# Mixing-stage range sums moved from ScalarE to VectorE, the first layer's input forms made later, and five more blocks computed by seven products

## The chip, the cores and the metric

The kernel runs on one core of one Trainium2 chip. The metric is device time in microseconds (us) of one execution. TensorE multiplies; VectorE, ScalarE and GpSimd work on its results; each engine takes its instructions strictly in the order in which they were written, and waits at the head of its queue until what the instruction needs is there.

## What is computed

One inference step of a one-layer hybrid decoder on 264 tokens: 256 prompt tokens and 8 sampled ones with a carried state. The layer is a half-step SwiGLU (feed-forward 1), a mixing block, and a second SwiGLU (feed-forward 2); a last RMSNorm follows. The reference, cut:

```python
D_MODEL, D_FF, SEQ, DEC_BATCH, H_A, DK = 2048, 5504, 256, 8, 4, 256

def swiglu(x, wg, wu, wd):
    return (jax.nn.silu(x @ wg) * (x @ wu)) @ wd

def mixing_block(h, w_in, b_gates, conv_w, conv_b, norm_mlstm, norm_conv, w_out, C0, n0, m0, buf0):
    z = h @ w_in
    q, k, v, o, ig, fg, gb, gc, xc = jnp.split(z, offs, axis=-1)
    ...
    ha, C_f, n_f, m_f = mlstm_chunkwise(qh, kh, vh, logi, logf, C0, n0, m0)   # 4 heads
    ha = ha * lax.rsqrt(jnp.mean(ha * ha, axis=-1, keepdims=True) + EPS)
    ha = ... * norm_mlstm * jax.nn.sigmoid(o)
    u = gc * xc                                   # short gated convolution, 3 taps
    yc = sum(cw[j] * u_ext[:, j:j + S] for j in range(CONV_W)) + conv_b
    yb = gb * yc                                  # normalised per group of 128 channels
    return jnp.concatenate([ha, yb], axis=-1) @ w_out, C_f, n_f, m_f, new_buf

h = h + 0.5 * swiglu(rmsnorm(h, norm_ffn1), ffn1_gate, ffn1_up, ffn1_down)
h = h + mixing_block(rmsnorm(h, norm_mix), ...)
h = h + 0.5 * swiglu(rmsnorm(h, norm_ffn2), ffn2_gate, ffn2_up, ffn2_down)
y = rmsnorm(h, norm_final)
```

Everything is float32 in memory; the weights (some 350 MB) are read once.

## The kernel before

**Layout.** Activations are kept transposed, channels on the 128 partitions and the 264 tokens along the free dimension. A weight matrix is cut into blocks of 128 output channels. A *product* is one such block: 16 contraction steps of 128 for an input of 2048 channels, and 22 or 21 steps for one half of the 5504 feed-forward channels. Feed-forward blocks j = 0 to 42 are worked in two halves (0 to 21 and 22 to 42): gate and up products of all blocks of the half, then the *down* products, 16 output blocks in 8 pairs (`db // 2` = 0 to 7), which add the half's share into `h`.

**Split numbers.** A float32 number is scaled and cut into two float16 numbers, high and low. For the weights ScalarE casts the high part (`high`, L240) and VectorE subtracts to get the low one (`low`, L248). Each product has three matmuls per contraction step (`three`, L322 to L324): high by high, high by low, low by high, each 264 columns. A weight tile `w` holds up to 8 steps. `fetch` (L254) issues the DMA of a raw tile, the cast, and the subtraction (with `lag` set, the subtraction waits until the next fetch); there are six buffers of `wraw` and of `w`, so the cast of a tile waits until TensorE has done with the tile six before.

**By seven.** Some blocks are computed in pairs by `product_pair` (L361): gate and up of one block (`GU_SEVEN`), or two down blocks (`DOWN_SEVEN`, keyed by layer and half, listing `db // 2`). The high-by-high matmuls stay as they are (264 columns, L387). The two correction terms are replaced, for every two contraction steps, by seven products of half the tokens (132 columns, two matmuls each, L371 and L372). For that VectorE must make four sums of weight tiles per pair of tiles (`weight_sums`, L301, tile `s`), sums of the input in *forms* (`token_sums`, L359: `f` of the layer's input, `g` of the activations), and put the results together (`join`, L427 to L437; in a down pair, `joined` then adds them to `h` at L869).

**Order of the work.** There is no scheduler: the order on each engine is that of the program. `tick()` advances a counter when a product begins, `tick(0.5)` half-way through, and `at(delta, f)` files the work `f` to be issued at a later tick; a pair counts as two products. So `at(1, norm.form, 0)` puts the forms one product later on VectorE's queue, and `Head` (L1174) and `Conv` (L1488) spread a head's or a convolution block's small steps over the products that follow theirs.

**Range sums.** The float16 cut holds only for numbers within a range. `watch` (L562) sums the absolute values of the last 16 columns of each result in PSUM into a column of `stat`; `join` does the like for pairs into `twins` (L437). At the end the sums are compared with bounds, and if one is out, the whole step is done again in full float32 (`hymba_step`, L142). In this kernel `watch` is one ScalarE activation with an accumulated output (L569, tile `seen`). It is called for every gate, up and down block not computed by seven, for every projection of the mixing block (`project`, L1033, after VectorE's scaled eviction at L1036), for the gates, for the 16 output blocks (`result`, L1605), and for the last two blocks.

**Mixing.** `MIX_ORDER` (L82) interleaves four heads (6 products each), eight convolution blocks (3 each) and eight output gates. For each head, ScalarE squares 16 columns of the sampled outputs at tick 12.5 (`squares`, L1471, activation at L1473) and TensorE sums them at tick 13.5 (`norm`, L1475, through `column_sums`, L673).

Of the kernel before, what the change touches and what calls it, by code (L numbers as in the profile page):

```python
# [8 lines left out]
F32 = mybir.dt.float32  # L9
# [3 lines left out]
AF = mybir.ActivationFunctionType  # L13
ALU = mybir.AluOpType
# [36 lines left out]
GU_SEVEN = {  # L51
    n: [j for half in starts for j in half]
    for n, starts in (
        ("1", (range(7, 21, 2), range(22, NFB - 1, 2))), ("2", (range(5, 21, 2), range(22, NFB - 1, 2))),
    )
}
DOWN_SEVEN = {("1", 0): (1, 3, 5, 7), ("1", 1): (1, 3, 5), ("2", 0): (1, 3, 5, 7), ("2", 1): (1, 3)}
PAIRS = sum(len(v) for v in GU_SEVEN.values()) + sum(len(v) for v in DOWN_SEVEN.values())
TH = T // 2

# [104 lines left out]
def step(ctx: ExitStack, tc: tile.TileContext, a: dict, shared, bad=None):  # L165
# [141 lines left out]
    def at(delta, fn, *args):  # L307
        agenda.setdefault(int(seq[0]) + delta, []).append((fn, args))
# [250 lines left out]
        onesb = const.tile([128, 128], BF16, name="onesb")  # L559
        nc.gpsimd.memset(onesb, 1.0)  # L560

    def watch(ps, rows=None):  # L562

        if half_size:
            j, n = len(stats), ps.shape[-1]
            stats.append(j)
            for r in rows or [slice(0, 128)]:
                seen = tmp.tile([128, SEEN], F32, tag="seen", name="seen", bufs=2)
                nc.scalar.activation(  # L569
                    seen[r], ps[r, n - SEEN : n], AF.Abs, accum_out=stat[r, j : j + 1]  # L570
                )

    def watch_norm(ssum):
# [191 lines left out]
    def ffn(layer, norm, done, start=None, end=None):  # L765
        with ExitStack() as stack:
# [55 lines left out]
            for half, blocks in enumerate(HALVES):  # L822
                act = {}
                def block(i, j):
                    nonlocal first
                    pg = gate_up(j, "g")
                    if first:
                        norm.finish()
                        first = False
                    zg = t264("ta")  # L830
                    nc.vector.tensor_tensor(zg, pg, norm.r, op=ALU.mult)  # L831
                    watch(pg)
                    sg = t264("tb")
                    nc.scalar.activation(sg, zg, AF.Silu)
                    pu = gate_up(j, "u")
                    zu = t264("tc")
                    nc.vector.tensor_tensor(zu, pu, norm.r, op=ALU.mult)
                    activated(j, i, zu, sg)
                    watch(pu)

                for i, j in enumerate(blocks):
                    if j in sevens:
                        by_seven(j, i)
                        continue
                    if first and start is not None:

                        ps4 = start()
                        for n, ps in enumerate(ps4):
                            early[n // 2, "gu"[n % 2]] = ps
                        for step, pairs in ((0, (0, 1)), (1, (2, 3)), (1.5, (4, 5)), (2, (6, 7))):  # L850
                            at(step, norm.square_pairs, fpool, pairs)
                        tick(0)
                        for which in "gu":
                            early[2, which] = product((layer, which, 2), norm.x, range(KB))
                    if half_size and j == (3 if start is not None else 1):
                        for g in range(2):
                            at(1 + g, norm.form, g)
                    lag[0] = half_size and j >= (3 if start is not None else 1)
                    if (j, "g") in early and not first:

                        at(j / 2 + 1, block, i, j)
                        continue
                    block(i, j)
# [14 lines left out]
                for db in range(0, KB - apart, 2):  # L878
# [5 lines left out]
                    for i in (db, db + 1):  # L884
# [3 lines left out]
                        )  # L888
                        if half == 1:
                            done(i)  # L890
                        watch(ps)
                lag[0] = False
                release()
                if apart:
# [810 lines left out]
```

## Time and profile before

| | |
|---|---|
| median of three runs | 1838.57 us (1837.24, 1838.57, 6681.73) |
| profiled execution, its own time | 1840.21 us |
| span in the profile | 1838.5 us, 44896 instructions |
| mean granted TensorE clock | 0.993 of full |
| TensorE busy (matmuls) | 1798.1 us, 98% |
| VectorE busy | 1525.3 us, 83% |
| ScalarE busy | 912.0 us, 50% |
| GpSimd busy | 140.4 us, 8% |
| HBM read | 366.72 MB, 206 GB/s read and written over the span |

By stage (from the stretches of the trace; busy us):

| stage | from to us | TensorE idle | VectorE | ScalarE |
|---|---|---|---|---|
| layer 1, gate and up, first half | 0 to 238 | 4.56 | 208.63 | 125.04 |
| layer 1, down, first half | 238 to 359 | 0.00 | 101.80 | 53.68 |
| layer 1, gate and up, second half | 359 to 572 | 0.25 | 196.33 | 96.86 |
| layer 1, down, second half | 572 to 690 | 0.00 | 102.32 | 56.82 |
| mixing, projections | 690 to 1070 | 23.85 | 283.52 | 229.91 |
| mixing, output blocks | 1070 to 1150 | 0.00 | 48.48 | 39.03 |
| layer 2, gate and up, first half | 1150 to 1371 | 0.28 | 194.13 | 103.34 |
| layer 2, down, first half | 1371 to 1494 | 0.00 | 103.58 | 54.32 |
| layer 2, gate and up, second half | 1494 to 1705 | 0.24 | 194.46 | 96.12 |
| layer 2, down, second half, and the end | 1705 to 1838.5 | 11.26 | 92.07 | 56.83 |

A row of the trace gives start and duration in us, engine, line, operation, output and inputs by the program's names, and in brackets how long the engine sat idle before it and whose instruction ended that. The granted clock is the share of full speed at which TensorE was allowed to run. One of the three runs took 6681.73 us; the repeat in float32 is the one branch of the program that could add so much, but that run has no profile.

### The profile page before, as it was taken

To read this page: it belongs to the slowest core of one execution; us is meant where nothing else is said; L and a number is where in the kernel's file an instruction comes from. 1 tells how busy PE (TensorE), PEld (TensorE's weight loads), DVE (VectorE), ACT (ScalarE), POOL (GpSimd) and SP (SyncE) were. 2 spreads that over 40 slices of the span, in tenths; PEclk is the share of its full clock that TensorE was granted. 3 is DMA by queue.
4 is the path that set the end of the run, shared out by engine and by line. 5 is a ranking of instruction groups with operands and counts; after the bars stand their busy time and mean duration, and the time that the engine had idled before them with its cause. 6 is when DMAs were issued, how large, how long until landed. Compare 5 with 4: busy or idle time off the path is not lost.

```text
span 1838.5 us, 44896 instructions
## 1 busy us (share of the span) xinstructions
PE 1798.1 (98%) x18780; PEld 1600.2 (87%) x18780; DVE 1525.3 (83%) x2371; ACT 912.0 (50%) x1738; POOL 140.4 (8%) x200
## 2 busy tenths in 40 slices
PE   9999999999999999989989999999999999999997
PEld 8899889999998987877878888899988999998886
DVE  7889988899998986777777766789988899999875
ACT  7544444444444544566656654544454444444542
POOL 0000000000000232211111022000000000000131
PEclk9999999999999999999999999999999999999999
DMA  8556666666666665877767666666666666666663
GB/s 300 185 184 203 196 221 194 210 204 199 200 191 206 201 203 179 294 251 248 242 226 254 202 204 200 196 195 186 205 211 199 200 207 197 193 207 195 213 200 100
DMA packets 118517, 381.51 MB, mean 208 GB/s; under 512 B 14973, under 2 KB 24797, under 8 KB 118305
## 3 DMA queue, kind: packets, MB, share of 16 engines
q1 hardware_dynamic: 109104, 350.53, 60.0%
q0 software_dynamic: 8256, 27.57, 4.4%
q8 instruction: 149, 2.44, 0.5%
q10 hardware_dynamic: 944, 0.45, 0.1%
q14 instruction: 64, 0.52, 0.1%
HBM read 366.72 MB, written 11.78 MB: 206 GB/s over the span
## 4 chain that ended last, share of the span: by engine, by line
PE 74%; DVE 11%; ACT 7%; issue 5%; DMA 1%; SPq 0%; ACTq 0%; DVEq 0%; POOL 0%; POOLq 0%
PE ps L324 16%; PE ps L322 16%; PE ps L323 16%; PE ps L387 10%; PE ps L371 8%; PE ps L372 8%; DVE w L248 4%; ACT w L240 3%; DVE s L301 1%; ACT jk L1465 1%; DMA wraw<-in_w1gu 1%; ACT cs L1437 1%; ACT seen L569 1%; DVE jk L1457 0%; DVE qkv L1036 0%
## 5 line engine op out<-in xcount | busy, mean ns | idle before, releaser
L248 DVE SCALAR_TENSOR_TENSOR w<-wraw,w 128x1024 f16<-128x1024 f32 (+3 forms) x692 | 800.6, 1181 | 159.6 <-ACT w L240 158.3
L240 ACT ACTIVATE w<-wraw 128x1024 f16<-128x1024 f32 (+3 forms) x692 | 665.3, 1007 | 115.1 <-issue 57.6
L324 PE MATMUL ps<-x,w 128*128 128x264 f16 x1568 | 433.6, 277 | 3.3 <-DVE w L248 3.3
L322 PE MATMUL ps<-x,w 128*128 128x264 f16 x1568 | 433.6, 277 | 0.0
L323 PE MATMUL ps<-x,w 128*128 128x264 f16 x1568 | 433.5, 276 | 0.0
L324 PEld LDWEIGHTS <-w 128*128 128x128 f16 x3576 | 350.8, 98 | 63.7 <-DVE w L248 9.6
L322 PEld LDWEIGHTS <-w 128*128 128x128 f16 x3576 | 351.3, 98 | 55.1 <-ACT w L240 3.0
L323 PEld LDWEIGHTS <-w 128*128 128x128 f16 x3576 | 350.9, 98 | 53.4 <-issue 0.3
L324 PE MATMUL ps<-xm,w 128*128 128x264 f16 x896 | 249.3, 278 | 3.3 <-DVE w L248 3.3
L322 PE MATMUL ps<-xm,w 128*128 128x264 f16 x896 | 249.4, 278 | 2.5 <-ACT w L240 2.5
L323 PE MATMUL ps<-xm,w 128*128 128x264 f16 x896 | 249.3, 278 | 0.0
L322 PE MATMUL ps<-a,w 128*128 128x264 f16 (+2 forms) x856 | 227.7, 271 | 0.0
L323 PE MATMUL ps<-a,w 128*128 128x264 f16 (+2 forms) x856 | 227.7, 271 | 0.0
L324 PE MATMUL ps<-a,w 128*128 128x264 f16 (+2 forms) x856 | 227.6, 271 | 0.0
L569 ACT ACTIVATE seen<-ps 128x16 f32<-128x16 f32 (+1 forms) x214 | 37.5, 175 | 331.3 <-DVE ta L831 132.2
L387 PEld LDWEIGHTS <-w 128*128 128x128 f16 x1682 | 162.0, 98 | 22.8
L372 PEld LDWEIGHTS <-s 128*128 128x128 f16 x1672 | 162.2, 97 | 0.0
L371 PEld LDWEIGHTS <-s 128*128 128x128 f16 x1672 | 161.3, 96 | 0.0
L301 DVE TENSOR_TENSOR s<-s,w 128x1024 f16<-128x1024 f16 (+2 forms) x218 | 146.0, 670 | 3.8
L301 DVE TENSOR_TENSOR s<-w 128x1024 f16<-128x1024 f16 (+2 forms) x218 | 138.2, 675 | 4.0
L387 PE MATMUL ps<-x,w 128*128 128x264 f16 x1120 | 137.4, 276 | 0.0
L372 PEld LDWEIGHTS <-w 128*128 128x128 f16 x1264 | 123.3, 98 | 1.7
(272 smaller groups left out, 2275.1 us busy)
## 6 DMA issues: line engine op xcount, KB each, us to landing
wraw<-in_w2gu SPq DMA_DIRECT2D x172, 512.0 KB, 4.7
wraw<-in_w1gu SPq DMA_DIRECT2D x164, 512.0 KB, 4.6
wraw<-in_win SPq DMA_DIRECT2D x112, 512.0 KB, 5.2
wraw<-in_w2d SPq DMA_DIRECT2D x52, 448.0 KB, 4.1
wraw<-in_w1d SPq DMA_DIRECT2D x46, 448.0 KB, 4.0
wraw<-in_w1d SPq DMA_DIRECT2D x36, 512.0 KB, 4.5
wraw<-in_wout SPq DMA_DIRECT2D x32, 512.0 KB, 4.6
wraw<-in_w2d SPq DMA_DIRECT2D x32, 512.0 KB, 4.5
```

Source lines behind the costliest of these rows:

```text
L240: nc.scalar.activation(dst, src, AF.Copy, scale=scale)
L248: nc.vector.scalar_tensor_tensor(dst, src, scale, hi, op0=ALU.mult, op1=ALU.subtract)
L301: nc.vector.tensor_tensor(s[:, out], x, y, op=ALU.add)
L322: nc.tensor.matmul(ps, wh, xk[:, 0, :], start=first, stop=False)
L323: nc.tensor.matmul(ps, wh, xk[:, 1, :], start=False, stop=False)
L324: nc.tensor.matmul(ps, wl, xk[:, 0, :], start=False, stop=last)
L371: nc.tensor.matmul(ps, w[0], x[:, 1], start=first, stop=False)
L372: nc.tensor.matmul(ps, w[1], x[:, 0], start=False, stop=last)
L387: nc.tensor.matmul(ps[:, :T], hi[:, i], xs[i][:, 0], start=(k0 + i == 0), stop=False)
L569: nc.scalar.activation(seen[r], ps[r, n - SEEN : n], AF.Abs, accum_out=stat[r, j : j + 1])
L1437: nc.scalar.activation(c[:, b], c[:, b], AF.Copy, scale=sib[:, 2 * n + b, self.hd : self.hd + 1])
L1465: nc.scalar.activation(self.jk[n][:, b, eb], self.jk[n][:, b, eb], AF.Copy, accum_out=ha[self.hd][:, eb, col : col + 1],)
```

## The change

Four edits:

- In the mixing block, for the output blocks and for the last two blocks, `watch` becomes a VectorE reduction (absolute values, 16 columns of PSUM, `tensor_reduce`). The feed-forward blocks keep the ScalarE form by `scalar=True`.
- In layer 1 the forms of the input are filed 4 and 6 ticks after block 3 begins; they were filed 1 and 2 ticks after.
- `DOWN_SEVEN` gains the pairs that take (1, 3, 5, 7) to (1, 3, 4, 6, 7), (1, 3, 5) to (1, 3, 4, 6), and in layer 2 (1, 3) to (1, 3, 4).
- `GU_SEVEN` of layer 2 starts at block 3, not 5.

By these tables 36 gate/up blocks and 17 down pairs are computed by seven; there were 35 and 13. (The few words that name the change speak of 18 down pairs; the table lists 17.)

```diff
-        ("1", (range(7, 21, 2), range(22, NFB - 1, 2))), ("2", (range(5, 21, 2), range(22, NFB - 1, 2))),
+        ("1", (range(7, 21, 2), range(22, NFB - 1, 2))), ("2", (range(3, 21, 2), range(22, NFB - 1, 2))),
...
-DOWN_SEVEN = {("1", 0): (1, 3, 5, 7), ("1", 1): (1, 3, 5), ("2", 0): (1, 3, 5, 7), ("2", 1): (1, 3)}
+DOWN_SEVEN = {
+    ("1", 0): (1, 3, 4, 6, 7), ("1", 1): (1, 3, 4, 6),
+    ("2", 0): (1, 3, 4, 6, 7), ("2", 1): (1, 3, 4),
+}
...
-    def watch(ps, rows=None):
+    def watch(ps, rows=None, scalar=False):
...
             for r in rows or [slice(0, 128)]:
-                seen = tmp.tile([128, SEEN], F32, tag="seen", name="seen", bufs=2)
-                nc.scalar.activation(
-                    seen[r], ps[r, n - SEEN : n], AF.Abs, accum_out=stat[r, j : j + 1]
+                if scalar:
+                    seen = tmp.tile([128, SEEN], F32, tag="seen", name="seen", bufs=2)
+                    nc.scalar.activation(
+                        seen[r], ps[r, n - SEEN : n], AF.Abs, accum_out=stat[r, j : j + 1]
+                    )
+                    continue
+                nc.vector.tensor_reduce(
+                    stat[r, j : j + 1], ps[r, n - SEEN : n], axis=mybir.AxisListType.X,
+                    op=ALU.add, apply_absolute_value=True,
                 )
...
-                    watch(pg)
+                    watch(pg, scalar=True)
...
                         for g in range(2):
-                            at(1 + g, norm.form, g)
+                            at((4 + 2 * g) if start is not None else (1 + g), norm.form, g)
```

The lines of the changed kernel stand 3 to 9 further down (L569 becomes L573, L1473 becomes L1482).

**ScalarE in the mixing block, at the squares of the second head.** The names are `jk` a product of state and query that is summed, `yb` a convolution block's output, `w` a weight tile, `ex` the decays, `sq` the squares. Before:

```order
L1465 ACTIVATE jk,ha_10388<-jk 128x256 x4
L240 ACTIVATE yb_10381<-yc 128x264
L240 ACTIVATE w<-wraw 128x1024 x2
L569 ACTIVATE seen,stat<-ps 128x16
L1253 ACT_TABLE_LOAD
L1253 ACTIVATE ex<-ex 128x256
L1253 ACTIVATE ex<-ex 128x128
L240 ACTIVATE w<-wraw 128x1024 x2
L1473 ACTIVATE sq_12653<-ha_10388 128x16
L569 ACTIVATE seen,stat<-ps 128x16
```

The same place of the changed kernel:

```order
L1474 ACTIVATE jk,ha_10552<-jk 128x256 x4
L243 ACTIVATE yb_10545<-yc 128x264
L243 ACTIVATE w<-wraw 128x1024 x2
L1262 ACT_TABLE_LOAD
L1262 ACTIVATE ex<-ex 128x256
L1262 ACTIVATE ex<-ex 128x128
L243 ACTIVATE w<-wraw 128x1024 x2
L1482 ACTIVATE sq_12789<-ha_10552 128x16
```

Only the range sums (`seen`) are gone from the queue; on VectorE a reduction into `stat` now follows each eviction of a projection.

**VectorE in layer 1, between the first evictions.** `ta` and `tc` are evicted gate and up products, `a` the activations, `f` the forms. Before:

```order
L837 TENSOR_TENSOR tc<-ps,rstd 128x264
L780 TENSOR_TENSOR tc<-tc,tb 128x264
L248 SCALAR_TENSOR_TENSOR a_682<-tc,a_682 128x264
L359 TENSOR_TENSOR f_687<-x_192 128x1056 x2
L359 TENSOR_TENSOR f_687<-f_687,x_192 128x1056
L359 TENSOR_TENSOR f_687<-x_192,f_687 128x1056
L248 SCALAR_TENSOR_TENSOR w<-wraw,w 128x1024
L831 TENSOR_TENSOR ta<-ps,rstd 128x264
```

In the changed kernel the first forms stand behind the eviction of block 4's gate:

```order
L789 TENSOR_TENSOR tc<-tc,tb 128x264
L251 SCALAR_TENSOR_TENSOR w<-wraw,w 128x1024
L251 SCALAR_TENSOR_TENSOR a_682<-tc,a_682 128x264 x2
L251 SCALAR_TENSOR_TENSOR w<-wraw,w 128x1024
L840 TENSOR_TENSOR ta<-ps,rstd 128x264
L362 TENSOR_TENSOR f_915<-x_192 128x1056 x2
L362 TENSOR_TENSOR f_915<-f_915,x_192 128x1056
L362 TENSOR_TENSOR f_915<-x_192,f_915 128x1056
L251 SCALAR_TENSOR_TENSOR w<-wraw,w 128x1024 x2
```

Six weight tiles and the evictions of blocks 1 to 3 have moved ahead of the first forms; the second forms follow one block later.

**VectorE in layer 1, second down half, from the last sums of pair 3 on.** `s` are the weight sums, `y` and `twins` belong to the join of pair 3, `h` is the residual. Before, pair 4 is two ordinary products:

```order
L301 TENSOR_TENSOR s<-s,w 128x2x256 x2
L248 SCALAR_TENSOR_TENSOR w<-wraw,w 128x896 x4
L430 TENSOR_TENSOR y_9573<-y_9573,ps 128x132
L431 TENSOR_TENSOR y_9573<-ps,y_9573 128x264
L434 TENSOR_TENSOR y_9573<-ps,y_9573 128x132
L435 TENSOR_TENSOR y_9573<-ps,y_9573 128x264
L436 TENSOR_TENSOR y_9573<-ps,y_9573 128x264
L437 TENSOR_REDUCE twins<-y_9573 128x2
L869 SCALAR_TENSOR_TENSOR h_81<-y_9573,h_81 128x528
L248 SCALAR_TENSOR_TENSOR w<-wraw,w 128x896
```

In the changed kernel pair 4 is by seven too. These rows begin behind the sums of its first two tiles:

```order
L304 TENSOR_TENSOR s<-s,w 128x1024 x2
L251 SCALAR_TENSOR_TENSOR w<-wraw,w 128x1024 x2
L304 TENSOR_TENSOR s<-w 128x1024 x2
L304 TENSOR_TENSOR s<-s,w 128x1024 x2
L433 TENSOR_TENSOR y_9668<-y_9668,ps 128x132
L434 TENSOR_TENSOR y_9668<-ps,y_9668 128x264
L437 TENSOR_TENSOR y_9668<-ps,y_9668 128x132
L438 TENSOR_TENSOR y_9668<-ps,y_9668 128x264
L439 TENSOR_TENSOR y_9668<-ps,y_9668 128x264
L440 TENSOR_REDUCE twins<-y_9668 128x2
L878 SCALAR_TENSOR_TENSOR h_81<-y_9668,h_81 128x528
L251 SCALAR_TENSOR_TENSOR w<-wraw,w 128x640 x2
```

The join of pair 3 now stands between the second and the third pair of tiles of pair 4, which TensorE needs next.

More of the change, by code (lines that the diff above doesn't have):

```diff
@@ L838, in block @@
                     activated(j, i, zu, sg)
-                    watch(pu)
+                    watch(pu, scalar=True)
                 for i, j in enumerate(blocks):
@@ L890, in ffn @@
                             done(i)
-                        watch(ps)
+                        watch(ps, scalar=True)
                 lag[0] = False
```

## The prediction

> **What bounds the kernel now.** I read the page's first table, then the stretches by stage and around the dips of the granted clock (TensorE, its weight loads, VectorE, ScalarE and GpSimd busy, clock, DMA):
>
> ```profile
> PE 1798.1 (98%) x18780; PEld 1600.2 (87%) x18780; DVE 1525.3 (83%) x2371; ACT 912.0 (50%) x1738; POOL 140.4 (8%) x200
> ...
> 55.00:70.00 15.00, 12.71 (x99) 10.18 (x98) 14.27 (x21) 8.98 (x20) 0.00 (x0) 0.89 0.63 203
> 790.00:822.00 32.00, 25.74 (x199) 21.21 (x197) 23.78 (x44) 21.28 (x53) 5.43 (x11) 0.95 0.79 273
> 868.00:890.00 22.00, 16.67 (x115) 13.62 (x114) 15.57 (x33) 10.31 (x21) 3.98 (x9) 0.84 0.61 189
> 948.00:970.00 22.00, 16.75 (x128) 13.91 (x127) 15.68 (x32) 10.54 (x19) 3.98 (x9) 0.84 0.53 172
> 238.00:359.00 121.00, 121.00 (x1374) 109.78 (x1372) 101.80 (x145) 53.68 (x81) 0.00 (x0) 1.00 0.65 211
> 572.00:690.00 118.00, 118.00 (x1256) 105.67 (x1254) 102.32 (x148) 56.82 (x100) 26.51 (x29) 1.00 0.66 206
> 690.00:1070.00 380.00, 356.15 (x3024) 303.24 (x3023) 283.52 (x514) 229.91 (x543) 57.07 (x101) 0.98 0.71 237
> ```
>
> TensorE is the bound: in the down stages it never rests, so only fewer matmuls help there. In the mixing block's projections it rests 380 - 356.15 = 23.85 us, though VectorE (283.52) and ScalarE (229.91) are far from full: something waits, nothing is overloaded. The waits of that stage (total, times, longest):
>
> ```profile
> PE ps L673 <- ACT sq L1473: 13.3, 4, 5.3
> PE ps L324 <- DVE w L248: 3.3, 5, 0.9
> PE ps L322 <- ACT w L240: 2.5, 2, 2.3
> ...
> DVE w L248 <- ACT w L240: 75.7, 48, 3.4
> ACT seen L569 <- DVE qkv L1036: 74.0, 24, 7.6
> ```
>
> ScalarE and VectorE wait for each other. One round of it, from the timelines around the stall at 870:
>
> ```profile
> 863.43 0.18 ACT L569 ACTIVATE seen<-ps 128x16 f32<-128x16 f32 x1 [4.35 <-DVE qkv L1036]
> 865.51 1.99 ACT L240 ACTIVATE w<-wraw 128x1024 f16<-128x1024 f32 x2
> 871.57 0.18 ACT L569 ACTIVATE seen<-ps 128x16 f32<-128x16 f32 x1 [4.07 <-DVE qkv L1036]
> 871.89 1.28 ACT L1253 ACT_TABLE_LOAD   x1
> 875.60 0.20 ACT L1473 ACTIVATE sq<-ha 128x16 f32<-128x16 f32 x1
> ...
> 866.59 2.36 DVE L248 SCALAR_TENSOR_TENSOR w<-wraw,w 128x1024 f16<-128x1024 f32 x2 [3.25 <-ACT w L240]
> 870.84 0.29 DVE L1249 TENSOR_TENSOR ex<-ex,bc 128x128 f32<-128x128 f32 x1
> 871.05 0.42 DVE L1036 TENSOR_TENSOR qkv<-ps,rstd 128x264 f32<-128x264 f32 x1
> ...
> 875.85 1.02 PE L673 MATMUL ps<-sq,ones 128*128 128x8 f32 x4 [5.33 <-ACT sq L1473]
> ```
>
> `seen` waits for VectorE's eviction, the casts stand behind `seen`, VectorE's subtractions wait for the casts, and the next eviction stands behind those. From one `seen` to the next is 871.57 - 863.43 = 8.14 us, for one projection. TensorE needs less for one, by the pieces of the chain of waits where it never stops:
>
> ```profile
> 87.81 1.80 PE ps L387 x16
> 92.83 1.80 PE ps L387 x16
> 108.65 1.80 PE ps L387 x16
> ```
>
> 16 matmuls of 264 columns take 1.80, so 0.1125 each, and a projection of 48 takes 5.4. ScalarE thus falls 2.7 us behind with such a round, until the squares are late and TensorE stands 5.33 us.
>
> **What a stall costs besides.** After the stalls the clock is below 1. Lost are, by the four stretches, (1 - 0.89) x 15 = 1.65, 0.05 x 32 = 1.6, and 0.16 x 22 = 3.5 twice; 8.6 of it in the mixing block. The Trainium skill, "TensorE: Matmul & The Clock Gate" (Part 1), has the clock halved after at least one idle window of about 3.4 us. Here the 2.29 us of 57 (its row is below) sufficed. By the page's length the first two of the four losses would not hang on their gaps and would stay, and the sum would be 3.3 us smaller; I go by the rows.
>
> **The range sums.** They leave ScalarE's queue; with `seen` gone the circle is cut, since neither a cast nor anything behind it waits for the eviction any more. ScalarE still waits for VectorE at `ex`, at the products `jk` and the convolution's inputs, but those were issued half a projection to one and a half earlier. For 870: without the waits of 4.35 and 4.07, `sq` is held by `ex`, which ended at 871.13 behind 3.25 us of waiting for casts; 867.9, then exponentials and casts as now (from the table load's end at 873.17 to 875.60, 2.4) give 870.3, against TensorE's asking at 870.52. It is just in time, with no credit for earlier rounds. I take away the squares' 13.3, the casts' 2.5, half of the subtractions' 3.3, and the clock's 8.6, and leave 0.5 a head, 2.0, for squares still late: 13.3 + 2.5 + 1.6 + 8.6 - 2.0 = 24.0.
>
> VectorE gets 58 reductions in this stage (56 projections, two for the gates). None of this form is in the trace. Nearest are
>
> ```profile
> L437 DVE TENSOR_REDUCE twins<-y 128x2 f32<-128x32 f32 x48 | 9.0, 188 | 1.6
> L592 DVE TENSOR_REDUCE downs<-ps 128x1 f32<-128x264 f32 x8 | 3.0, 422 | 0.0
> ```
>
> in size the first, from PSUM the second, which reads 264 columns. 58 x 0.188 = 10.9, at most 58 x 0.422 = 24.5. It goes into 283.5 of now 350 us, so up to 308 (88%): hidden, except where VectorE is last. I charge 2.0, some ten of them, and 0 to 10.9 for the range. Below nothing it can't be. Next late is VectorE itself, at the gates, whose part of the 23.85 (4.75, what the three waits don't hold) stays. Mixing: -24.0 + 2.0 = -22.0. The 16 sums of the output blocks and the two at the end (18 x 0.188 = 3.4) lie under matmuls; without that cover they cost that.
>
> **The forms of layer 1.** VectorE then TensorE:
>
> ```profile
> 55.32 1.32 DVE L359 TENSOR_TENSOR f<-x 128x1056 f16<-128x1056 f16 x2
> 57.29 0.71 DVE L359 TENSOR_TENSOR f<-x,f 128x1056 f16<-128x1056 f16 x1
> 57.92 1.22 DVE L248 SCALAR_TENSOR_TENSOR w<-wraw,w 128x1024 f16<-128x1024 f32 x1
> 71.65 0.43 DVE L831 TENSOR_TENSOR ta<-ps,rstd 128x264 f32<-128x264 f32 x1 [0.41 <-PE ps L324]
> ...
> 59.19 0.29 PE L324 MATMUL ps<-x,w 128*128 128x264 f16 x1 [2.29 <-DVE w L248]
> ```
>
> TensorE stands 2.29 us for the tile that is subtracted behind the second forms (55.32 to 57.92, 2.6). They and the first forms, as long, now come later, so the tile is there 2.6 to 5.2 us sooner: the stall and its 1.65 of clock go, -3.9. At 71.65 VectorE already waits for TensorE with the same work done, so the forms find room before block 7, their first user at 87.8. If not, the stall returns there at the same price.
>
> **Five more by seven.** Between 87.81 and 92.83 lies half a gate/up block by seven: 5.02, less 1.80 leaves 3.22 for 56 small matmuls, 0.0575 each. An ordinary block is 96 x 0.1125 = 10.80, one by seven 10.04: -0.76. A down pair of 22 steps: 132 x 0.1125 = 14.85 against 44 x 0.1125 + 154 x 0.0575 = 13.81, -1.04, twice; of 21 steps 14.18 against 46 x 0.1125 + 140 x 0.0575 = 13.23, -0.95, twice. Together -4.7. Their cover is VectorE's lead:
>
> ```profile
> 341.37 1.41 DVE L301 TENSOR_TENSOR s<-s,w 128x1024 f16<-128x1024 f16 x2
> 345.95 1.80 PE ps L387 x16
> 354.58 1.29 DVE L301 TENSOR_TENSOR s<-w 128x1024 f16<-128x1024 f16 x2
> 359.57 1.29 DVE L301 TENSOR_TENSOR s<-w 128x1024 f16<-128x1024 f16 x2
> 363.25 0.28 DVE L430 TENSOR_TENSOR y<-y,ps 128x132 f32<-128x132 f32 x1
> 365.76 4.62 DVE L248 SCALAR_TENSOR_TENSOR w<-wraw,w 128x1024 f16<-128x1024 f32 x4
> ...
> 630.36 0.88 DVE L301 TENSOR_TENSOR s<-s,w 128x512 f16<-128x512 f16 x2
> 631.06 0.73 PE L387 MATMUL ps<-a,w 128*128 128x264 f16 x5
> ```
>
> Sums were ready at 342.78; TensorE, starting the pair at 345.95, needs them after 1.80 and 24 x 0.0575, at 349.13: 6.3 us of lead. Subtractions and sums go at 359.57 - 354.58 = 4.99 a pair of tiles, TensorE at 5.02, so a run of sevens only loses the joins, 365.76 - 363.25 = 2.5 each. Where pairs 6 and 7 and block 22 now follow each other, two joins leave 1.3: no stall. In the second half of layer 1 the lead at the third tiles of pair 3 is smaller: sums at 631.24, needed 14 x 0.1125 + 12 x 0.0575 after 631.06, at 633.33, 2.1. One join ahead of pair 4's third tiles makes it -0.4, and the next tile's subtraction stands behind a cut of `xm`: I charge 1.5 there and 0.5 in layer 2, which cuts nothing; 0 to 6 for the range. Layer 2's block 3 uses forms made at block 1, as block 5 did. Net -2.7.
>
> **The sum.** -22.0 - 3.9 - 2.7 = -28.6 on the profiled execution's 1840.2 (span 1838.5 and 1.7 around it) gives 1811.6. That execution lay 1.6 above the median of 1838.57, so I forecast 1810.
>
> **The rivals.**
>
> *The circle loosens only.* ScalarE still waits for `ex`, `jk` and the taps; just in time at 870 may be just late. If a third of mixing's gain comes, 7.3: 1838.6 - 7.3 - 3.9 - 2.7 = 1825. Against it: 74.0 us of waiting had `seen` at its end, and the ties left reach back further.
>
> *The wait moves to VectorE.* The reductions lengthen the queue that the evictions stand in, by 10.9, and the squares stay late: mixing gives nothing, 1832. The Trainium skill, "VectorE: DVE Perf Modes" (Specifications), puts ScalarE nearer to PSUM and VectorE nearer to SBUF, which speaks for leaving the sums; no row here shows that distance. Against it: VectorE waits 75.7 us in this stage and has room for them.
>
> *VectorE becomes the bound in the down stages: slower than before.* In 238 to 359 it has 101.80; one pair more brings 2 x 4.99 + 3.8 for the short third of sums and subtractions, of which the subtractions (half) were there, and a join: some 9.5, 111 of 120. The margin of 1.3 at block 22 is the point: if sums run a fifth slower (beside GpSimd's squares, say), two pairs lose 2 x 2.8 us more and each of five places stalls 5 us and 1.7 of clock: 5 x 6.7 - 4.7 = +29. With the forms' -3.9 and a mixing block that, as in the case before, gives nothing, 1863. For it: the lead of 2.1 in the second half. Against it: 0.00 idle in these stages now.
>
> *Everything goes.* All 23.85 and 8.6 of mixing, with 3.9 and 4.7: -41, 1798. Against it: the gates' chain is VectorE's own.
>
> *The change doesn't do it.* A repeat of the whole step, should a VectorE sum fall out of its bounds, would cost thousands of us; the sums are of the same numbers. An 18th down pair, which the tables lack, would be worth about 1.0 more.
>
> **How the numbers follow.** Forecast 0.62 (1803 to 1818), loosened circle 0.18 (1819 to 1829), wait moved 0.08 (1830 to 1838), everything 0.06 (under 1803), VectorE the bound 0.05, repeat 0.01. The range takes the forecast's own and the loosened circle's, and half of "everything" below: 1801 to 1828, some 8 in 10. About 2% is what a measurement of this kernel can tell from no change; it lies at 1801.8 and 1875. Faster takes most of "everything", 0.05; slower the repeat and the tail of the VectorE case, 0.02; within, 0.93.
>
> **What would show it.** Right: the wait of L673 for the squares under 3 us, ScalarE's waits for `qkv` gone, VectorE's waits for casts in mixing well under 75.7, clock 1.00 from 868 to 970, no gap near 57 us, 17 joins in down pairs. Wrong: squares still late behind `ex`; TensorE waiting for `s` or `w` at pair 4 of layer 1's second half or at block 22; reductions much over 0.2 us.

## The result, and the profile after

The changed kernel takes 1811.72 us (median; 1811.32 to 1812.50) against 1838.57 us for the kernel before on the same chip. Two runs are left out of the medians and ratios here, one of the kernel before (6681.73 us) and one of the experiment with the first halves' tables taken back (10187.09 us), which have no profile. The ratio is 0.9856, with a 95% interval of 0.9837 to 0.9876: 26.5 us less (23 to 30), short of the 2% that were to be told from no change. The forecast was 1810 us. That the total came out is luck: three of its parts did not, and their errors cancel.

The first table of the page of the changed kernel, then its stretches around the place of the old stall at 57 us, over its mixing projections, and over its stall at 42 us (TensorE, weight loads, VectorE, ScalarE and GpSimd busy, granted clock, DMA):

```profile
PE 1784.7 (99%) x19080; PEld 1595.9 (88%) x19080; DVE 1572.0 (87%) x2528; ACT 896.0 (49%) x1571; POOL 145.9 (8%) x200
...
55.00:70.00 15.00, 15.00 (x136) 13.04 (x134) 14.41 (x23) 9.06 (x22) 0.00 (x0) 1.00 0.64 208
694.00:1031.00 337.00, 336.02 (x2934) 290.80 (x2934) 279.32 (x561) 214.72 (x419) 62.60 (x101) 1.00 0.78 263
41.00:50.00 9.00, 8.09 (x53) 6.27 (x54) 5.88 (x11) 5.26 (x11) 0.00 (x0) 0.81 0.42 130
```

TensorE now rests 337.00 - 336.02 = 0.98 us in the mixing projections, at full clock. What it waits for in the whole run of the changed kernel (total, times, longest), and VectorE's largest wait in the mixing projections:

```profile
PE ps L327 <- DVE w L251: 5.9, 9, 1.1
PE ps L682 <- DVE sq L748: 2.7, 1, 2.7
...
PE ps L390 <- ACT w L243: 1.1, 2, 0.5
PE ps L374 <- DVE s L304: 0.8, 2, 0.5
PE ps L459 <- ACT xm L243: 0.7, 1, 0.7
...
DVE w L251 <- ACT w L243: 24.5, 17, 3.4
```

The head's squares are no longer in the list. New are short waits, each at most 1.1 us, for VectorE's tiles `w` and `s`: these lie in the stages with more blocks by seven and in the second gate/up halves, which follow such stages.

The lengths of the stages, each from TensorE's first matmul that reads the stage's input to that of the next stage (for example `x` after `a` for the second gate/up half), in us:

| stage | before | after | difference | forecast |
|---|---|---|---|---|
| start and layer 1 gate/up, first half | 244.74 | 244.86 | +0.12 | -3.9 |
| layer 1 down, first half | 114.85 | 113.80 | -1.05 | -1.04 |
| layer 1 gate/up, second half | 219.63 | 222.08 | +2.45 | 0 |
| layer 1 down, second half | 110.87 | 113.25 | +2.38 | +0.55 |
| mixing projections and output blocks | 455.87 | 422.96 | -32.91 | -22 |
| layer 2 gate/up, first half | 232.42 | 232.78 | +0.36 | -0.76 |
| layer 2 down, first half | 114.85 | 113.80 | -1.05 | -1.04 |
| layer 2 gate/up, second half | 219.61 | 222.15 | +2.54 | 0 |
| layer 2 down, second half, and the end | 125.66 | 125.02 | -0.64 | -0.45 |
| span | 1838.5 | 1810.7 | -27.8 | -28.6 |

So mixing gave 10.9 us more than forecast, the five added pairs (four of down blocks, and gate and up of one block) cost 5.0 us where 2.7 were to be gained, and in this execution the first stage became no shorter.

### The profile page after: what moved, and what is told of

Same layout as the page of the kernel before. It is cut to its first block, busy times and chain, and to the rows that moved or that the text cites. A ratio compares the mean times of both kernels' runs of the same rounds, so it can differ in the third digit from the quotient of the medians.

```text
span 1810.7 us, 45495 instructions
## 1 busy us (share of the span) xinstructions
PE 1784.7 (99%) x19080; PEld 1595.9 (88%) x19080; DVE 1572.0 (87%) x2528; ACT 896.0 (49%) x1571; POOL 145.9 (8%) x200
## 3 DMA queue, kind: packets, MB, share of 16 engines
q8 instruction: 151, 2.47, 0.5%
## 4 chain that ended last, share of the span: by engine, by line
PE 74%; DVE 17%; ACT 4%; issue 3%; DMA 1%; SPq 0%; ACTq 0%; DVEq 0%
PE ps L327 17%; PE ps L325 17%; PE ps L326 17%; PE ps L390 8%; PE ps L374 7%; PE ps L375 7%; DVE w L251 6%; DVE s L304 5%; ACT w L243 3%; DMA wraw<-in_w1gu 1%; DVE g L362 1%; DVE a L251 1%; DVE y L821 1%; PE ps L682 0%; DVE y L434 0%
## 5 line engine op out<-in xcount | busy, mean ns | idle before, releaser
L327 PE MATMUL ps<-x,w 128*128 128x264 f16 x1536 | 424.9, 277 | 4.6 <-DVE w L251 4.6
L325 PE MATMUL ps<-x,w 128*128 128x264 f16 x1536 | 424.9, 277 | 0.0
L326 PE MATMUL ps<-x,w 128*128 128x264 f16 x1536 | 424.8, 277 | 0.0
L327 PEld LDWEIGHTS <-w 128*128 128x128 f16 x3372 | 330.2, 98 | 56.9 <-DVE w L251 8.5
L326 PEld LDWEIGHTS <-w 128*128 128x128 f16 x3372 | 330.2, 98 | 49.7
L325 PEld LDWEIGHTS <-w 128*128 128x128 f16 x3372 | 330.4, 98 | 48.4 <-issue 0.6
L390 PEld LDWEIGHTS <-w 128*128 128x128 f16 x1886 | 181.1, 98 | 27.0 <-ACT w L243 1.8
L374 PEld LDWEIGHTS <-s 128*128 128x128 f16 x1872 | 180.0, 96 | 2.3 <-DVE s L304 2.2
L375 PEld LDWEIGHTS <-s 128*128 128x128 f16 x1872 | 181.7, 97 | 0.0
L327 PE MATMUL ps<-a,w 128*128 128x264 f16 (+2 forms) x684 | 180.2, 269 | 1.4 <-DVE w L251 1.4
L325 PE MATMUL ps<-a,w 128*128 128x264 f16 (+2 forms) x684 | 180.2, 269 | 0.0
L326 PE MATMUL ps<-a,w 128*128 128x264 f16 (+2 forms) x684 | 180.2, 269 | 0.0
L304 DVE TENSOR_TENSOR s<-s,w 128x1024 f16<-128x1024 f16 (+2 forms) x246 | 164.8, 670 | 4.3
L304 DVE TENSOR_TENSOR s<-w 128x1024 f16<-128x1024 f16 (+2 forms) x246 | 156.5, 677 | 5.3
L390 PE MATMUL ps<-x,w 128*128 128x264 f16 x1152 | 141.8, 276 | 1.1 <-ACT w L243 1.1
L375 PEld LDWEIGHTS <-w 128*128 128x128 f16 x1418 | 138.3, 98 | 2.5 <-DVE w L251 0.4
L374 PEld LDWEIGHTS <-w 128*128 128x128 f16 x1418 | 138.1, 97 | 2.0
```

Of the source, the lines that this page charges most:

```text
L304: nc.vector.tensor_tensor(s[:, out], x, y, op=ALU.add)
L325: nc.tensor.matmul(ps, wh, xk[:, 0, :], start=first, stop=False)
L326: nc.tensor.matmul(ps, wh, xk[:, 1, :], start=False, stop=False)
L327: nc.tensor.matmul(ps, wl, xk[:, 0, :], start=False, stop=last)
L374: nc.tensor.matmul(ps, w[0], x[:, 1], start=first, stop=False)
L375: nc.tensor.matmul(ps, w[1], x[:, 0], start=False, stop=last)
```

## The experiments

Each kernel below was timed beside new runs of the kernel before on the same chip. The stages carry the arguments, since a stage without change repeats from run to run within some 0.1 us; only the start (240 to 245 us) and the mixing projections without their stall (335.7 to 339.3 us) vary more.

**Each edit alone.** The range sums only, with the feed-forward blocks kept on ScalarE as in the change:

```diff
...
-                seen = tmp.tile([128, SEEN], F32, tag="seen", name="seen", bufs=2)
-                nc.scalar.activation(
-                    seen[r], ps[r, n - SEEN : n], AF.Abs, accum_out=stat[r, j : j + 1]
+                nc.vector.tensor_reduce(
+                    stat[r, j : j + 1], ps[r, n - SEEN : n], axis=mybir.AxisListType.X,
+                    op=ALU.add, apply_absolute_value=True,
                 )
...
```

> The kernel before with the range sums of the mixing on VectorE, and nothing else of the change. Theory (the sums cut the whole circle of ScalarE's wait for the subtraction, the squares' stall and the lowered clock): the stages of the mixing and of the output blocks lose 33 us together as they do in the changed kernel, so about 1806 us. Rival (the sizes of the prediction, which left 2 us of stalls, took 2 us for the reductions, and counted half of the subtractions): -22 us, about 1817. Rival that the wait moves to VectorE: about 1838.

Measured: 1807.68 us, ratio 0.9831 (0.9814 to 0.9847), 31 us less (28 to 34). The mixing and its output blocks take 335.99 + 86.40 us where they took 367.51 + 88.36: 33.5 us less. The prediction's size of 22 is outside.

The five pairs by seven only:

```diff
-("2", (range(5, 21, 2), range(22, NFB - 1, 2))),
+("2", (range(3, 21, 2), range(22, NFB - 1, 2))),
-DOWN_SEVEN = {("1", 0): (1, 3, 5, 7), ("1", 1): (1, 3, 5), ("2", 0): (1, 3, 5, 7), ("2", 1): (1, 3)}
+DOWN_SEVEN = {("1", 0): (1, 3, 4, 6, 7), ("1", 1): (1, 3, 4, 6), ("2", 0): (1, 3, 4, 6, 7), ("2", 1): (1, 3, 4)}
```

> The kernel before with the five added pairs of blocks by seven, and nothing else of the change. Theory (a third pair in a row spends VectorE's lead, and the following half of gate/up blocks does not give it back): the profile shows 2 to 2.5 us more in the second gate/up halves and in the down blocks of the first layer's second half, 1 us less in the down blocks of the first halves, in all about +5 us: about 1843 us. Rival (the prediction): -2.7 us, about 1836 us.

Measured: 1845.03 us, ratio 1.0036 (1.0022 to 1.0051), 6.7 us more (4 to 9). The stages repeat those of the changed kernel: first down halves 113.80 and 113.81, second gate/up halves 222.09 and 222.17, layer 1's second down half 113.28.

The later forms only:

```diff
-                            at(1 + g, norm.form, g)
+                            at((4 + 2 * g) if start is not None else (1 + g), norm.form, g)
```

> The kernel before with the two forms of x later in the first layer, and nothing else of the change. Theory: the stall of 2.29 us about 57 us after the start goes, and with it the half clock behind it: -3.9 us, about 1834.7 us. Rival (the start is set by the loads of the weights, which land as late or later, and the stall only moves ahead): within 1 us of 1838.6.

Measured: 1833.67 us, ratio 0.9978 (0.9968 to 0.9987), 4.1 us less (2 to 6). Its first stage takes 240.72 us, 4.0 less than before, and in the stretch of the old stall TensorE does not rest:

```profile
55.00:70.00 15.00, 15.00 (x135) 13.04 (x134) 14.66 (x22) 9.06 (x20) 0.00 (x0) 1.00 0.70 225
```

The changed kernel without the five pairs, that is sums and forms together:

> The changed kernel with the kernel before's tables of pairs by seven (no fifth pair in any half, gate/up blocks of the second layer from block 5). Theory (the five pairs cost about 5 us net): about 1806.5 us or less, which beats the changed kernel. Rival (the prediction, the five pairs bring 2.7 us): about 1814.4 us.

Measured: 1803.74 us, ratio 0.9814 (0.9798 to 0.9831). The changed kernel came to 0.9856 (and 0.9839 when run again, below): without the pairs it is faster. Its edit is the second diff, taken back from the changed kernel.

**What the mixing block waited for.** Two kernels go out from the kernel before and leave everything but the mixing's range sums alone. One leaves these out:

```diff
         nc.vector.tensor_tensor(z, ps, nm.r, op=ALU.mult)
-        watch(ps)
         return z
```

> The kernel before with the 56 range sums of the mixing's projections left out altogether (their columns of the range test keep the value they are set to at the start, so that part of the test is not computed); those of the gates and of the output blocks stay on ScalarE. Beside the kernel with the sums alone on VectorE (ratio 0.983, projections of the mixing 336.0 us where before took 367.5) it gives the price of the 56 reductions on VectorE. Theory (ScalarE's wait was the cost and the reductions lie beside other work): 336 us again, about 1807 to 1810 us. Rival (VectorE's queue is paid for, 56 x 0.165 us): 9 us less than that kernel, 327 us for the stage, about 1799 us.

Measured: 1807.53 us, ratio 0.9840 (0.9825 to 0.9855); mixing projections 337.19 us, against 335.99 with the sums on VectorE. The rival's 327 us is out; a price below the 3.6 us by which this stage varies can't be told. The other keeps them on ScalarE and writes each one projection later:

```diff
         nc.vector.tensor_tensor(z, ps, nm.r, op=ALU.mult)
-        watch(ps)
+        waiting.append(ps)
+        if len(waiting) > 1:
+            watch(waiting.pop(0))
         return z
...
         for ob in last:
             Gate(ob)
+        while waiting:
+            watch(waiting.pop(0))
```

> The kernel before with the mixing's 56 range sums still on ScalarE, each written one projection later, behind the next projection's eviction, so that ScalarE has the same work and finds the eviction done. Theory (the wait for the eviction, not ScalarE's 0.17 us for a sum, made the circle): most of the 31.5 us of the stage goes, 336 to 342 us for it, 1807 to 1813 us in all. Rival (the work itself was too much for ScalarE, or the eviction is still waited for one projection later): 360 us or more for the stage, 1830 to 1838 us.

Measured: 1809.38 us, ratio 0.9846 (0.9831 to 0.9861); mixing projections 338.82 us, so 28.7 of the 31.5 us are gained with the sums still on ScalarE. Its groups of ScalarE in the stretch from 690 to 1027 us (count, busy time, mean ns, idle time before them and what ended it), first in the kernel before:

```profile
L240 ACT ACTIVATE w<-wraw 128x1024 f16<-128x1024 f32 x100 | 99.8, 1048 | 0.1
...
L569 ACT ACTIVATION_READ_ACCUMULATOR seen<-ps 128x1 f32 x50 | 9.7, 194 | 0.0
L569 ACT ACTIVATE seen<-ps 128x16 f32<-128x16 f32 x50 | 9.1, 182 | 131.6 <-DVE qkv L1036 74.0 <-DVE ta L1036 30.2 <-DVE tb L1036 19.5
```

and with the sums one projection later:

```profile
L240 ACT ACTIVATE w<-wraw 128x1024 f16<-128x1024 f32 x113 | 114.2, 1047 | 15.5 <-PE ps L324 14.4 <-DMA wraw<-in_win 0.9
...
L569 ACT ACTIVATION_READ_ACCUMULATOR seen<-ps 128x1 f32 x56 | 11.0, 196 | 0.0
L569 ACT ACTIVATE seen<-ps 128x16 f32<-128x16 f32 x56 | 9.5, 170 | 12.4 <-DVE qkv L1038 6.4 <-DVE ta L1038 5.9
```

The sums cost the same 0.37 us each and there are more of them, since the block goes faster. What is gone is the wait ahead of them, 131.6 us against 12.4. Casts now wait for TensorE (14.4 us), that is for a free tile: ScalarE is ahead. Its queue order was the cost, not its work.

No price of VectorE's reductions shows. Their group in the mixing projections of the changed kernel, and the stretch from 690 to 1027 us with the sums on VectorE and with no sums:

```profile
L577 DVE TENSOR_REDUCE stat<-ps 128x1 f32<-128x16 f32 x55 | 9.0, 164 | 0.0
```

```profile
690.00:1027.00 337.00, 336.61 (x2940) 291.02 (x2938) 278.26 (x560) 214.60 (x419) 61.06 (x101) 1.00 0.79 261
```

```profile
690.00:1027.00 337.00, 335.69 (x2921) 290.05 (x2910) 273.16 (x502) 215.27 (x423) 64.08 (x101) 1.00 0.77 260
```

With 9.0 us of reductions more, TensorE is not less busy (336.61 against 335.69).

**Where the added pairs lose.** The changed kernel once more, and three variants of its tables, ran on one chip.

> The changed kernel once more, beside the three that follow. It should repeat its ratio of 0.986. What is open is its start: in its profile the first layer's first half of gate/up blocks took 244.9 us, while the two kernels with the later forms alone and with the forms and the sums took 240.7 and 241.8. Theory (the loads of that one execution came late): this profile shows 241 to 242 us there. Rival (the tables of pairs make the start later): again near 245 us.

Measured: 1809.64 us, ratio 0.9839 (0.9823 to 0.9856). Its start took 242.44 us and stands near the first expectation; the variants' starts, with the same first half of layer 1, took 244.10, 240.46 and 241.04 us. So the start varies from execution to execution with the tables of that half the same. What differs in the traces is TensorE's wait from some 39 us on for `sq` (the stall at 42), the squares of the layer's input that VectorE adds up: 2.68 us in the changed kernel, 2.62 when run again, 2.52 in the first variant, none in the second and 0.28 in the third. The squares stand behind casts in ScalarE's queue, and the casts wait for weight tiles to land. These waits up to 45 us, of the changed kernel and of the spread kernel further below, whose start took 240.24 us:

```profile
ACT w L243 <- DMA wraw<-in_w1gu: 7.8, 10, 2.0
```

```profile
ACT w L240 <- DMA wraw<-in_w1gu: 4.6, 8, 1.6
```

The wait for `sq` does not come from the later forms: it is 2.03 us with the five pairs alone and 2.34 with the sums one projection later. That late tiles cause it is read from the traces, not tried, and why they land later in some executions is open.

```diff
-    ("1", 0): (1, 3, 4, 6, 7), ("1", 1): (1, 3, 4, 6),
-    ("2", 0): (1, 3, 4, 6, 7), ("2", 1): (1, 3, 4),
+    ("1", 0): (1, 3, 5, 7), ("1", 1): (1, 3, 4, 6),
+    ("2", 0): (1, 3, 5, 7), ("2", 1): (1, 3, 4),
```

> The changed kernel with the first halves' down pairs by seven as before (1, 3, 5, 7), so that no three pairs by seven follow each other at pairs 6 and 7 and block 22. Theory (the third pair in a row spends VectorE's lead, which 220 us of gate/up blocks don't give back): the second gate/up halves lose their 2.5 us each, the down halves gain back 1.05 each, so 1811.7 - 5.0 + 2.1 = 1808.8 us, and less where the second down halves profit. Rival (the stalls in the second gate/up halves come from something else): 1811.7 + 2.1 = 1813.8 us.

Measured: 1807.21 us, ratio 0.9820 (0.9801 to 0.9840). The second gate/up halves, which themselves are unchanged, fall back to 219.67 and 219.66 us.

```diff
-("1", (range(7, 21, 2), range(22, NFB - 1, 2))), ("2", (range(3, 21, 2), range(22, NFB - 1, 2))),
+("1", (range(7, 21, 2), range(24, NFB - 1, 2))), ("2", (range(3, 21, 2), range(24, NFB - 1, 2))),
```

> The changed kernel with all five added pairs, but without the first block by seven of each second gate/up half (they start at block 24, no longer at 22). Theory (one ordinary block, in which VectorE has no sums of weights to make, gives the lead back): the stalls in the second gate/up halves go, -2.5 us each, and the two ordinary blocks cost 0.76 us each, so 1811.7 - 5.0 + 1.5 = 1808.2 us, and down to 1805 if the second down halves' stalls go too. Rival (the lead is not what is missing): 1811.7 + 1.5 = 1813.2 us.

Measured: 1806.39 us, ratio 0.9819 (0.9802 to 0.9835). The second gate/up halves take 220.42 us each: 219.65 + 0.77, an ordinary block in place of one by seven and no stall. (Layer 1's second down half stays at 113.24: its stall is another.) In that block VectorE waits for TensorE; its rows are

```profile
359.86 0.43 DVE L840 TENSOR_TENSOR ta<-ps,rstd 128x264 f32<-128x264 f32 x1 [1.10 <-PE ps L327]
...
365.26 0.43 DVE L846 TENSOR_TENSOR tc<-ps,rstd 128x264 f32<-128x264 f32 x1 [2.14 <-PE ps L327]
```

so it has caught up within one block.

```diff
-("1", 1): (1, 3, 5), ("2", 0): (1, 3, 5, 7), ("2", 1): (1, 3)}
+("1", 1): (1, 3, 5), ("2", 0): (1, 3, 5, 7), ("2", 1): (1, 3, 4)}
```

(against the kernel with sums and forms)

> The changed kernel with one added pair of the five, the one in the second layer's second half (1, 3, 4); the other tables as before the change. By the stages this pair alone was worth something, 0.6 us: 1803.7 - 0.6 = 1803.1 us. If its gain hung on a queue that the other pairs had moved: 1803.7 to 1805 us.

Measured: 1803.66 us, ratio 0.9807 (0.9791 to 0.9824). The last stage takes 125.13 us, 0.5 less than the 125.67 without that pair; the whole times can't show so little.

From it the last two kernels go out. Five pairs in the first halves, but otherwise placed:

```diff
-DOWN_SEVEN = {("1", 0): (1, 3, 5, 7), ("1", 1): (1, 3, 5), ("2", 0): (1, 3, 5, 7), ("2", 1): (1, 3, 4)}
+DOWN_SEVEN = {("1", 0): (1, 2, 4, 5, 7), ("1", 1): (1, 3, 5), ("2", 0): (1, 2, 4, 5, 7), ("2", 1): (1, 3, 4)}
```

> The kernel of the run with one added pair (1803.7 us), and in the first halves five pairs by seven placed 1, 2, 4, 5, 7 instead of four at 1, 3, 5, 7: as many as the changed kernel has there, but with an ordinary pair ahead of pair 7, so that only pair 7 and block 22 follow each other at the end. Theory (what counts is three in a row ahead of the gate/up half, not the number): the first down halves take 113.80 us, the second gate/up halves stay at 219.65 us, 2.1 us less in all: 1801.6 us. Rival (any fifth pair spends the lead): second gate/up halves of 222.1 us, 1803.7 - 2.1 + 4.9 = 1806.5 us.

Measured: 1800.37 us, ratio 0.9799 (0.9786 to 0.9813). The first down halves take 113.80 and 113.81 us, as with the changed kernel's tables, and the second gate/up halves 219.67 and 219.68, as before the change. It is the fastest kernel here, 2.0% below the kernel before (1.9 to 2.1). By the stages, the five spread pairs bring 1.05 us in each layer.

Rows of VectorE and TensorE at the seam show it. The four subtractions behind the last pair's join, and TensorE's start of the half, of the kernel before stand at 365.76 (its row is in the prediction) and

```profile
359.59 0.61 PE L387 MATMUL ps<-x,w 128*128 128x264 f16 x4
...
549.96 0.42 DVE L780 TENSOR_TENSOR y<-y,tb 128x264 f32<-128x264 f32 x1
...
557.83 0.29 PE L324 MATMUL ps<-x,w 128*128 128x264 f16 x1 [0.25 <-DVE w L248]
```

and of the changed kernel at

```profile
358.66 1.51 PE L390 MATMUL ps<-x,w 128*128 128x264 f16 x12
...
367.40 4.62 DVE L251 SCALAR_TENSOR_TENSOR w<-wraw,w 128x1024 f16<-128x1024 f32 x4
...
473.77 0.29 PE L327 MATMUL ps<-x,w 128*128 128x264 f16 x1 [0.48 <-DVE w L251]
...
551.48 0.42 DVE L789 TENSOR_TENSOR y<-y,tb 128x264 f32<-128x264 f32 x1
...
553.50 1.07 PE L390 MATMUL ps<-x,w 128*128 128x264 f16 x8 [0.54 <-ACT w L243]
...
559.36 0.29 PE L327 MATMUL ps<-x,w 128*128 128x264 f16 x1 [1.09 <-DVE w L251]
```

From the stage's start VectorE comes out of its joins 6.17 us late before (365.76 - 359.59) and 8.74 us late after (367.40 - 358.66): 2.57 more. Some 184 us later, at the same product `y` of a block near the half's end, it is 190.37 and 192.82: 2.45 more. The delay was carried through the whole half, and TensorE paid it in one stall half-way (0.48 us at 473) and in those near the end. In the spread kernel, whose half starts at 240.24 + 113.80 = 354.04, the four subtractions stand at

```profile
360.21 4.62 DVE L248 SCALAR_TENSOR_TENSOR w<-wraw,w 128x1024 f16<-128x1024 f32 x4
```

that is 6.17 us late again, with as many pairs by seven. VectorE's one kind of wait between 360 and 480 us is for casts, with the same total, count and longest in the kernel before and in the changed one; it never waits for TensorE there, so TensorE's pace does not bound it and it has no way to make up time:

```profile
DVE w L248 <- ACT w L240: 7.4, 15, 1.5
```

```profile
DVE w L251 <- ACT w L243: 7.4, 15, 1.5
```

Yet VectorE is not full there: it is busy for 110.69 of these 120 us in the changed kernel. Each of the 15 casts that it waits for, in both kernels, stands in ScalarE's queue behind a wait for VectorE itself (for `ta`, `tc` or `y`). One such round of the changed kernel:

```profile
421.46 0.42 DVE L840 TENSOR_TENSOR ta<-ps,rstd 128x264 f32<-128x264 f32 x1
421.91 0.18 ACT L573 ACTIVATE seen<-ps 128x16 f32<-128x16 f32 x1 [3.34 <-DVE ta L840]
422.71 1.99 ACT L243 ACTIVATE w<-wraw 128x1024 f16<-128x1024 f32 x2
423.79 1.23 DVE L251 SCALAR_TENSOR_TENSOR w<-wraw,w 128x1024 f16<-128x1024 f32 x1 [0.43 <-ACT w L243]
```

So the two engines hold each other here as they did in the mixing block, and the delay goes round with them. The activation `tb` behind `seen` reads the same `ta`, so moving the range sum alone would not open this round. Whether casts written ahead of that wait would give the lead back was not tried.

Last, a fourth pair in layer 1's second half at another place:

```diff
-DOWN_SEVEN = {("1", 0): (1, 2, 4, 5, 7), ("1", 1): (1, 3, 5), ...
+DOWN_SEVEN = {("1", 0): (1, 2, 4, 5, 7), ("1", 1): (1, 3, 5, 6), ...
```

> The kernel of the spread run (1800.4 us) with a fourth pair by seven in the first layer's second half at 6, so 1, 3, 5, 6: two in a row as in the changed kernel, but at another place and after an ordinary pair 4. In the spread run the sums of pair 5's third tiles are ready at 653.6 and used at 655.2, a lead of 1.6 us, against 2.2 at pair 3. Theory (in this half any second pair in a row overdraws a lead of about 2 us by its join and its cut of the mixing's input): these down blocks take 113 us or more, no longer 110.87, and the whole 1802.5 to 1804 us. Rival (the stall hung on the place 4): 109.9 us there, 1799.4 us in all.

Measured: 1805.03 us, ratio 0.9828 (0.9811 to 0.9844); these down blocks take 112.87 us, 0.1 less than was expected at the least, 2.0 more than with three pairs, and far from the 109.9 of the rival. The whole is 1 us above the expected range; its start took 242.04 us, 1.8 more than in the spread kernel. The idle times of TensorE in that half, first of the changed kernel, where pairs 3 and 4 follow each other,

```profile
648.87 0.23 PE L374 MATMUL ps<-g,s 128*128 128x132 f16 x1 [0.36 <-DVE s L304]
649.76 0.23 PE L374 MATMUL ps<-g,s 128*128 128x132 f16 x1 [0.48 <-DVE s L304]
651.62 0.29 PE L327 MATMUL ps<-a,w 128*128 128x264 f16 x1 [0.78 <-DVE w L251]
```

then with pairs 5 and 6:

```profile
671.57 0.23 PE L371 MATMUL ps<-g,s 128*128 128x132 f16 x1 [0.36 <-DVE s L301]
672.46 0.23 PE L371 MATMUL ps<-g,s 128*128 128x132 f16 x1 [0.48 <-DVE s L301]
674.33 0.29 PE L324 MATMUL ps<-a,w 128*128 128x264 f16 x1 [0.78 <-DVE w L248]
```

The same three waits of the same lengths come at the end of the second pair of the two, wherever it stands.

## Why the prediction was right, and where its steps were not

**What bounds the kernel: right.** TensorE is busy for 99% of the span after, and a first down half, in which it never waits, became shorter by just its saved matmuls.

**The circle of range sums: right in its mechanism, mis-sized.** In the changed kernel's profile ScalarE's waits for `qkv` are gone, the squares are not late, the clock of the mixing stays at 1.00, and the sums one projection later show that the order in ScalarE's queue was the cause. The term was 22.0, measured were 32.9. The forecast took less than the rows gave in four places, each time wrongly. The 2.0 left for squares still late: none were (in one later kernel, with block 22 ordinary, TensorE waited 0.79 us for them, once). Half of the subtractions' 3.3: all went, since VectorE is held less by late casts (its wait for them fell from 75.7 to 24.5). The 2.0 charged for the reductions: no price shows, and one took 0.164 us, not 0.188. And the 4.75 called the gates' chain was not that: in the stretch that the prediction read, the waits of the kernel before beside those it quoted were

```profile
PE ps L323 <- DVE xa L248: 1.8, 1, 1.8
PE ps L1317 <- issue: 1.6, 1, 1.6
PE ps L1146 <- DVE rows L1132: 0.6, 1, 0.6
PE ps L673 <- ACT sq L1536: 0.5, 1, 0.5
```

Only the 0.6 for `rows` belongs to the gates; the 1.8 stood in the output blocks, which went from 88.36 to 86.40 us. All four are gone after. Taken in full, 23.85 of idle time and 8.6 of clock are 32.45: the rival "everything goes" was right for this stage, and the reason against it ("the gates' chain is VectorE's own") was the misread row.

**The forms: right, but not seen in this execution.** Alone they gave 4.0 us in their stage where 3.9 were forecast, and the stall at 57 us is gone after, with clock 1.00. The profiled execution lost as much again at 42 us: 2.7 us of waiting for VectorE's `sq` and a clock of 0.81 over 9 us, another 1.7. In the spread kernel's profile that stall does not occur (start 240.24). Of the 3.9, the 2.29 of waiting is sure to go with the stall; the 1.65 of clock is not always there to be saved, since two kernels with the earlier forms had the same stall at full clock (last section).

**The five pairs: the step on the lead failed.** The savings by counted matmuls were right to 0.01 us where no stall came: -1.05 for a pair of 22 steps against -1.04. The step "two joins leave 1.3: no stall" was true at block 22 and useless: no stall came there. It ended at the seam, while the lead is also needed in the 220 us behind it. There a block by seven and an ordinary one alternate, VectorE keeps its delay from one to the next, and the half of the kernel before already ended with a wait for `w` of 0.25 us (at 557.83). So it had next to nothing to spare, and a delay at its start is a delay at its end: 2.45 and 2.54 us in the two layers, where 0 was forecast. Taking one block by seven out, or putting an ordinary pair ahead of pair 7, removes it.

In layer 1's second half the forecast had the place and the cause (the lead of about 2 us at the second pair of two, "the next tile's subtraction stands behind a cut"), but not the size: 1.5 us was charged, and 2.38 + 0.95 = 3.3 measured. The profile puts 2.0 of it down to waits for `s` and `w`, at pair 4 and behind pair 6; the rest is time between matmuls that it puts down to none. Layer 2's last half gave 0.64 (0.45 forecast). Block 3 of layer 2 cost 0.36 where 0.76 was to be gained, so 1.1 of stall; the trace has one wait of 1.09 us in that half, near its end, for a tile `w`. That it is the same lack of lead is argued from the two second halves, not tried.

**The sum.** Forecast -28.6, measured -27.8 in the profiled execution: mixing 10.9 better, the pairs 7.7 worse, the forms hidden for 4.0. The chances had no case for "mixing gives everything, and the pairs cost": of the rivals, "VectorE becomes the bound" had its right neighbour (a lead that is missing), at the wrong place and priced at +29 where +5.0 came.

## What to carry to other kernels

An in-order engine that waits for another at the head of its queue loses all that stands behind: before moving the work to another engine or counting its cost, try writing the same instruction later. If a stall of the bounding engine hangs on a circle, the whole of it can go, as here: check each leftover by its own row. Where one engine runs ahead of another, follow the lead to the next place at which it is rebuilt: in a stretch where the helping engine never waits for the bounding one, what is spent at its start can be due at its end, as in both layers here, and where a dear pair is placed can matter more than how many there are.

## What the runs showed of the hardware that was not expected

A sum of absolute values over 16 columns of PSUM takes ScalarE two instructions, 0.17 to 0.18 us for the activation and 0.19 to 0.20 for reading its accumulator, and VectorE one of 0.164 us.

Waits of TensorE of 2.29, 2.47 and 2.68 us (the kernel before at 57, the sums alone at 57, the changed kernel at 42) were each followed by a lowered clock: (1 - 0.89) x 15 = 1.65 and (1 - 0.81) x 9 = 1.7 us twice, the same for all three. Waits as long were also followed by full clock: 2.47 us in the kernel with the sums one projection later, at the same stall as that of the sums alone, 2.46 us there in the kernel without the sums, and 2.62 us in the changed kernel when run again. What decides it is not shown. After single waits up to 1.09 us, and after one of 1.77 (the kernel with a fourth pair at 6, at 39), the clock was full. The same stretch of the sums alone and of the sums one projection later, then of the changed kernel around its wait of 1.09 us:

```profile
57.00:66.00 9.00, 6.53 (x44) 5.01 (x44) 8.93 (x13) 4.57 (x11) 0.00 (x0) 0.81 0.52 159
```

```profile
58.50:67.50 9.00, 6.53 (x59) 5.68 (x59) 8.93 (x13) 4.57 (x11) 0.00 (x0) 1.00 0.50 155
```

```profile
559.00:566.00 7.00, 6.64 (x59) 5.79 (x60) 6.40 (x13) 3.72 (x5) 0.00 (x0) 1.00 0.67 207
```

The Trainium skill, "TensorE: Matmul & The Clock Gate" (Part 1), has the clock lowered after at least one idle window of about 3.4 us; here gaps of 2.3 to 2.7 us sufficed in some executions and not in others.
